# Moving a 64-token sample, and its cached keys and values, from the second super-block of a streaming encoder step to the first

## The chip, the cores and the metric

The kernel runs on one core of one Trainium2 chip. Its time is the device time in microseconds of one execution. The kernel before was run three times: 1246.68, 1248.00 and 1247.45 us, so its median is 1247.45 us.

## What is computed

The reference is one inference step of an encoder layer with two groups of heads that share one input projection. It is applied to 2048 new frames of one stream (the prompt) and, separately, to the next 64 frames of a running stream (the sample), which brings 512 cached rows of keys and values and a recurrent state:

```python
def mixer_layer(x, ln_g, w_in, lb, norm_g, w_out, attn_fn, s0):
    aq, ak, av, ag, hq, hf, hi, hg = jnp.split(rms_norm(x, ln_g) @ w_in, SPLITS, axis=-1)
    o_a = attn_fn(heads(aq), k, v).reshape(B, T, W_A) * jax.nn.silu(ag)
    o_b, S = hgrn2_branch(hq, hf, hi, hg, lb, norm_g, s0)
    y = x + jnp.concatenate([o_a, o_b], axis=-1) @ w_out
```

Group A is attention with 8 heads of 64: each chunk of 64 frames sees its own chunk and the 8 chunks ahead of it, so a prompt frame needs up to 512 earlier frames' keys and values, and the first 512 frames of the prompt have none before frame 0. The sample's 64 frames see the 512 cached rows and themselves. Group B is a gated linear recurrence with 4 heads of 128, whose gate is `f = lb + (1 - lb) * sigmoid(hf)`. `w_in` has 1024 x 4096 elements and `w_out` 1024 x 1024; everything is float32.

## The kernel before, in words

**Super-blocks and jobs.** The 2048 prompt tokens go through in four super-blocks of 512 (table SUPER, L37). The 64 sample tokens ride with one of them, as columns 512 to 575 of its tokens; before, that is the second. For each super-block the normalised tokens lie transposed in SBUF as a high part xh and a low part xl (the float32 value is split in two, so that three passes of matmuls in the faster float32r form give the product). The 32 jobs of a super-block (JOBS, L46; `project`) are the 32 column tiles of w_in: each runs 24 matmuls (8 contraction tiles, times high by high, low by high, high by low) into one of two PSUM accumulators called acc. A super-block of 512 tokens is one block of 512 columns for most jobs; the first two jobs and the last run in two halves of 256. With 576 tokens every job runs as a block of 256 and one of 320, because 512 columns is the most that one accumulator holds.

**Weights.** In the first super-block each tile of w_in is loaded raw (512 KB, two staging buffers wraw), cast to its high part by VectorE, subtracted to its low part by GpSimd in four pieces of 256 columns (`w_split`), and written to DRAM as 1 MB (wd) for the three super-blocks after it, which only load it (four buffers w). The first four raw tiles are loaded at once at the start: two in the wraw buffers, two in the rooms kd and v, which are not in use yet.

**Start.** `program` loads the gain row, the first four token tiles (three in the xn buffers, the fourth in the room kd), the first weights, and issues short matmuls on constants ("breath", "ident") till the first tokens are there. `x_tile` then does, for a tile of 128 tokens: a sum of squares on ScalarE, two small ScalarE instructions for the reciprocal root, two multiplications on VectorE, eight transposes on TensorE in two groups of four, and, in `x_split`, for each group a cast to xh on ScalarE and a subtraction to xl on VectorE. The first two jobs (hq and hf of head 0) are run by halves: half 0 of both, then half 1 of both. Half 1 needs all tiles of tokens from 256 on. `forget_bounds` computes lb and 1 - lb from lb_gamma in a handful of small instructions; the evacuation of hf (`ev_f`) uses them.

**Attention of a pair of heads** (`pair_jobs`, `attention`): kd holds 512 carried key columns and then the block's own, v four carried tiles of values and then the block's own. From the second super-block on, the carried part is loaded from DRAM (`carry`), where the super-block before had stored it. kd and v have one buffer each; the token `kv` passes them from pair to pair. In the first super-block their carried part is not used. For the sample, `sample_cache` loads the pair's cached keys and values (two transfers of 256 KB), transposes the keys on TensorE and splits both; before, it puts them in the two wraw buffers, which are free from the second super-block on. `sample_a` then attends with the sample's rows, after the pair's own blocks.

**Order.** All engines are scheduled by hand: generators (threads) yield a condition or a time, and the class Plan keeps a clock of its own with costs per instruction, resumes whichever thread is ready by that clock, and so writes out the order in which each engine's queue is filled. When the program runs, each engine works through its queue in that order, with semaphores where operands demand it. SyncE's queue holds nearly all DMA issues, in the same manner.

**The end.** The output projection (w_out in seven products per pair of 256-token blocks) fills the last part; the sample's rows are read back from DRAM (mixd) and projected there (`sample_load`, `out_sample`).

## Time and profile before

| What | Value |
|---|---|
| median of three runs | 1247.45 us (1246.68 to 1248.00) |
| span of the profiled execution, first to last instruction | 1244.9 us |
| TensorE: matmul busy, share of span | 1230.1 us, 99% |
| VectorE | 889.3 us, 71% |
| ScalarE | 701.5 us, 56% |
| GpSimd | 372.8 us, 30% |
| DMA | 273.29 MB, mean 220 GB/s |

The profiled execution is shown by its span; around it lies what the timed figure holds besides, 2.55 us if the profiled execution was like the median run. PE is TensorE's matmul queue, PEld its weight loads, DVE VectorE, ACT ScalarE, POOL GpSimd, SP SyncE (SPq its queue of DMA issues). A row of a group reads: engine, operation, output <- inputs by the program's names, shapes, count | busy us, mean ns of one | idle time of the engine just before them and what ended it. A row of the timeline reads: start, duration of the run of instructions, engine, operation, count, and in brackets the idle time before it with its releaser. A matmul's duration holds its way through the array; matmuls follow one another in less than that, so a pace is read from the starts of runs. All instructions of a queue have line L266, the helper that records them, so groups go by the names of tiles.

By the matmuls' names and starts, the first super-block's jobs run from 10 to 239 us, the second's to 546, the third's to 806 and the last one's to 1056.

### The profile page before, as it was taken

How to read it: one execution, taken by the hardware profiler on the slowest of the kernel's cores; microseconds unless marked ns; L12 is line 12 of the kernel's file. 1: busy time of each engine (PE TensorE's matmuls, PEld its weight loads, DVE VectorE, ACT ScalarE, POOL GpSimd, SP SyncE). 2: the span in 40 equal slices, each digit the busy share in tenths (PEclk: the TensorE clock that was granted, in tenths of full speed). 3: DMA queues.
4: the chain of work that ended last, by engine and by line, in shares of the span. 5: the costliest groups of instructions: out<-in, count | busy, mean ns of one | idle time of the engine just before them, and what ended most of it. 6: DMA issues, size and time to landing. Idle time of an engine off the chain costs nothing.

```text
span 1244.9 us, 22078 instructions
## 1 busy us (share of the span) xinstructions
PE 1230.1 (99%) x8068; PEld 1078.4 (87%) x8068; DVE 889.3 (71%) x1863; ACT 701.5 (56%) x1535; POOL 372.8 (30%) x699
## 2 busy tenths in 40 slices
PE   9999999999999999999999999999999999999997
PEld 8788888999999999998888888998888888888786
DVE  7678769776857578586584748683848574787886
ACT  6353556665655557575565657763636455644443
POOL 7757565111120210202543535100101204441110
PEclk9999999999999999999999999999999999999999
DMA  7788698645353553636859595846463656896431
GB/s 295 257 299 298 228 334 330 223 153 183 142 194 137 203 186 145 215 127 239 277 209 333 211 365 213 290 155 213 137 225 116 227 197 269 310 316 201 128 135 68
DMA packets 95406, 273.29 MB, mean 220 GB/s; under 512 B 10369, under 2 KB 43137, under 8 KB 77634
## 3 DMA queue, kind: packets, MB, share of 16 engines
q1 hardware_dynamic: 95154, 271.62, 62.0%
q8 instruction: 64, 1.05, 0.3%
q14 instruction: 44, 0.36, 0.1%
q10 hardware_dynamic: 144, 0.26, 0.1%
HBM read 188.23 MB, written 85.19 MB: 220 GB/s over the span
## 4 chain that ended last, share of the span: by engine, by line
PE 76%; DVE 5%; issue 2%; DMA 2%; ACT 2%; POOL 1%; SPq 0%; DVEq 0%; ACTq 0%; POOLq 0%
PE acc L266 55%; PE g L266 6%; PE tr L266 5%; PE pv L266 5%; PE s L266 5%; DMA wraw<-in_w_in_dram 1%; DVE xn L266 1%; DVE pr L266 1%; POOL w L266 1%; DMA xn<-in_x_prompt_dram 1%; ACT ck L266 0%; DVE q L266 0%; DMA So<-in_state_hgrn_dram 0%; DVE k L266 0%; ACT sig L266 0%
## 5 line engine op out<-in xcount | busy, mean ns | idle before, releaser
L266 PE MATMUL acc<-xh,w 128*128 128x512 f32 (+2 forms) x2688 | 567.2, 349 | 1.5 <-ACT sig L266 0.8
L266 PEld LDWEIGHTS acc<-xh,w 128*128 128x128 f32 x2688 | 434.4, 189 | 52.5 <-DVE gq L266 1.1
L266 PE MATMUL acc<-xl,w 128*128 128x512 f32 (+2 forms) x1344 | 296.2, 350 | 0.0
L266 PEld LDWEIGHTS acc<-xl,w 128*128 128x128 f32 x1344 | 217.2, 189 | 24.8
L266 DVE CUSTOM_DVE_ANT_0 pr<-s,bias 128x640 f32<-128x640 f32 (+5 forms) x144 | 100.8, 704 | 34.1 <-PE s L266 33.6
L266 ACT ACTIVATE pr<-pr,nm 128x640 f32<-128x640 f32 (+4 forms) x132 | 100.6, 763 | 40.6 <-DVE nm L266 39.6
L266 ACT CAST ph<-tr 128x512 fp32r<-128x512 f32 (+3 forms) x176 | 88.2, 507 | 62.4 <-PE tr L266 33.7
L266 POOL TENSOR_TENSOR w<-wraw,w 128x256 fp32r<-128x256 f32 x120 | 105.2, 906 | 54.4 <-issue 22.4
L266 POOL TENSOR_TENSOR mixa<-mixa,sga 128x256 f32<-128x256 f32 (+1 forms) x36 | 28.1, 783 | 308.5 <-DVE mixa L266 267.0
L266 DVE TENSOR_TENSOR ph<-tr,ph 128x512 fp32r<-128x512 f32 (+3 forms) x176 | 100.6, 590 | 8.6 <-ACT ph L266 7.4
L266 PE MATMUL pv<-ph,v 128*128 128x256 f32 (+2 forms) x344 | 95.7, 370 | 0.5 <-DVE ph L266 0.5
L266 PE MATMUL tr<-ident,pr 128*128 128x128 f32 x580 | 90.6, 273 | 0.4 <-DVE sig L266 0.2
L266 PEld LDWEIGHTS tr<-ident,pr 128*128 128x128 f32 x580 | 70.9, 140 | 13.7 <-issue 2.2
L266 ACT ACTIVATE sig<-acc 128x256 f32<-128x256 f32 (+2 forms) x86 | 42.7, 497 | 61.7 <-PE acc L266 61.5
L266 DVE TENSOR_SCALAR pr<-pr,sm 128x640 f32<-128x640 f32 (+4 forms) x132 | 72.9, 552 | 4.7
L266 ACT COPY vT<-acc 128x512 f32<-128x512 f32 (+2 forms) x62 | 31.0, 500 | 75.8 <-PE acc L266 75.7
L266 DVE TENSOR_TENSOR mixa<-mixa,pv 64x256 f32<-64x256 f32 (+1 forms) x144 | 56.9, 395 | 20.6 <-ACT mixa L266 16.4
L266 PEld LDWEIGHTS pv<-ph,v 128*128 128x128 f32 x344 | 58.2, 189 | 7.2 <-DVE ph L266 0.9
L266 ACT ACTIVATE sig<-sig 128x512 f32<-128x512 f32 (+2 forms) x109 | 57.4, 528 | 9.9 <-DVE gk L266 7.1
L266 POOL TENSOR_TENSOR xn<-wraw,xn 128x256 fp32r<-128x256 f32 x48 | 37.1, 792 | 69.5 <-ACT xn L266 69.5
L266 PE MATMUL s<-kd,q 128*128 128x320 f32 (+3 forms) x232 | 56.8, 315 | 0.4
L266 PE MATMUL s<-kd,ql 128*128 128x320 f32 (+3 forms) x232 | 55.5, 309 | 0.0
(314 smaller groups left out, 2041.8 us busy)
## 6 DMA issues: line engine op xcount, KB each, us to landing
w<-wd SPq DMA_DIRECT2D x96, 1024.0 KB, 5.0
wd<-w SPq DMA_DIRECT2D x32, 1024.0 KB, 7.7
wraw<-in_w_in_dram SPq DMA_DIRECT2D x30, 512.0 KB, 5.7
wod<-xn SPq DMA_DIRECT2D x28, 512.0 KB, 5.5
xn<-in_x_prompt_dram SPq DMA_DIRECT2D x23, 512.0 KB, 5.8
bias<-biasd SPq DMA_DIRECT2D x12, 640.0 KB, 7.0
carry<-kd SPq DMA_DIRECT2D x12, 512.0 KB, 6.2
carry<-v SPq DMA_DIRECT2D x12, 512.0 KB, 6.5
```

Source lines behind the costliest of these rows:

```text
L266: r = f(*args, **kw)
```

## The change

SUPER gives the first super-block 576 tokens and the second 512. What belongs to the sample follows: its tokens are a fifth tile of 64 rows at the start, loaded into a part of the room v; its cached keys and values go into the carried parts of kd and v (columns 0 to 511 and tiles 0 to 3) in place of the two wraw buffers; the output stage reads them from mixd[0]. `ev_f` waits, in the plan, till lb and 1 - lb have been issued ("forget") where it waited for an earlier step of theirs ("bounds"). The gain of a tile with 64 rows is cut to 64 rows.

```diff
 SUPER = [
-    (0, 512, [(0, 512)], [(0, 256), (256, 256)]),
-    (512, 576, [(0, 256), (256, 320)], [(0, 256), (256, 320)]),
+    (0, 576, [(0, 256), (256, 320)], [(0, 256), (256, 320)]),
+    (512, 512, [(0, 512)], [(0, 256), (256, 256)]),
     (1024, 512, [(0, 512)], [(0, 256), (256, 256)]),
     (1536, 512, [(0, 512)], [(0, 256), (256, 256)]),
 ]
...
         dve.tensor_scalar(oml, lb, -1.0, 1.0, ALU.mult, ALU.add)
+        have.add("forget")
         sp.dma_start(g_norm, hg_norm_g)
...
-            g = gain[k0 // 4] if gain else g_in[:rows]
+            g = gain[k0 // 4][:rows] if gain else g_in[:rows]
...
     def sample_cache(d):
         p = d.p
-        yield from tk["raw"].get()
-        yield from tk["raw"].get()
-        kc = T(px, [P, 2, 512], F32R, "wraw", bufs=RAWB)
-        vc = T(px, [P, 4, 4, 64], F32R, "wraw", bufs=RAWB)
...
-        yield from split_k(pt, kc, 0, 512, t)
+        yield from split_k(pt, d.kd, 0, 512, t)
...
-        yield from split_v(cv, vc, 0, 4, P, tv)
+        yield from split_v(cv, d.v, 0, 4, P, tv)
...
-        spans = [(kc, 0, 512), (kd, 512 + c0, DEC)]
+        spans = [(kd, 0, 512), (kd, 512 + c0, DEC)]
...
-        tk["raw"].put(2)
...
-            yield lambda: "bounds" in have and front()
+            yield lambda: "forget" in have and front()
...
-        sp.dma_start(mr, mixd[1][:, :, WIN : WIN + DEC].rearrange("f p t -> p f t"))
+        sp.dma_start(mr, mixd[0][:, :, WIN : WIN + DEC].rearrange("f p t -> p f t"))
...
-        xr0 = [T(px, [P, D], F32, "xn", bufs=XNB) for _ in range(3)] + [kroom[:, :D]]
+        xr0 = [T(px, [P, D], F32, "xn", bufs=XNB) for _ in range(3)] + [kroom[:, :D], vroom[:, D : 2 * D]]
...
-        for what, i in (("g", 0), ("x", 0), ("x", 1), ("w", 0), ("x", 2), ("w", 1), ("x", 3), ("b", 0), ("w", 2),
-                        ("w", 3)):
+        for what, i in (("g", 0), ("x", 0), ("x", 1), ("w", 0), ("x", 2), ("w", 1), ("x", 3), ("x", 4),
+                        ("b", 0), ("w", 2), ("w", 3)):
...
-                sp.dma_start(xr0[i], x_rows(0, i * P, P))
+                rows = min(P, SUPER[0][1] - i * P)
+                sp.dma_start(xr0[i][:rows], x_rows(0, i * P, rows))
...
-            for c in range(4):
-                C.spawn(x_tile(0, c // 2, c * P, (xr0[c], landed["x", c]), gps), 0)
+            for c in range(5):
+                C.spawn(x_tile(0, min(c // 2, 1), c * P, (xr0[c], landed["x", c]), gps), 0)
```

The program counts 7330 TensorE, 1355 ScalarE and 474 SyncE instructions before and after; VectorE has 1866 in place of 1865 and GpSimd 721 in place of 704, the 17 being short memsets of "breath" that the plan strews between its longer ones. What differs is the order.

**VectorE near the start**, before. xl is the low part of the tokens: xl from tr_313 and tr_325 is the third tile, from g_339 and acc_356 the fourth. lb and oml are the gate's bounds, w_387 and w_403 the weights of the third and fourth job, sig_389 the evacuation of hf's first half.

```order
L266 TENSOR_TENSOR xl_157<-g_339,xh_156 128x4x128
L266 TENSOR_TENSOR lmx_271<-le_272 128x4
L266 RECIPROCAL lmx_271<-lmx_271 128x4
L266 TENSOR_TENSOR lb_84<-le_272,lmx_271 128x4
L266 TENSOR_SCALAR oml_85<-lb_84 128x4
L266 TENSOR_TENSOR xl_157<-acc_356,xh_156 128x4x128
L266 CAST w_387<-kd_169 128x1024
L266 CAST w_403<-v_170 128x1024
L266 TENSOR_SCALAR sig_389<-sig_389,oml_85,lb_84 128x256
L266 TENSOR_SCALAR gk_308<-sig_389 128x256
L266 CAST w_435<-wraw_289 128x1024
```

The same place now. g_346 and acc_389 are the fourth tile, acc_399 and tr_404 the fifth; sig_385, gb_310, bm_411 and bl_412 belong to hf and the recurrence of head 0; w_435 is the third job's weight.

```order
L266 TENSOR_SCALAR oml_85<-lb_84 128x4
L266 TENSOR_SCALAR sig_385<-sig_385,oml_85,lb_84 128x256
L266 TENSOR_SCALAR gk_309<-sig_385 128x256
L266 TENSOR_TENSOR xl_157<-acc_389,xh_156 128x4x128
L266 SCALAR_TENSOR_TENSOR gb_310<-reset_80,sig_385 128x256
L266 TENSOR_TENSOR bm_411<-gb_310 128x256
L266 TENSOR_TENSOR xl_157<-acc_399,xh_156 128x4x64
L266 TENSOR_TENSOR bl_412<-gb_310 128x256
L266 TENSOR_TENSOR xl_157<-tr_404,xh_156 128x4x64
L266 CAST w_435<-kd_169 128x1024
L266 TENSOR_TENSOR q_129_418<-q_129_418,gq_308 128x256
L266 CAST w_448<-v_170 128x1024
```

Five instructions of head 0's gate and recurrence moved from behind the token tiles to between and ahead of them, and the casts of the third and fourth job's weights moved behind all of these.

**GpSimd, a little later**, before: the low parts of the third and fourth job's weights (four pieces each; the first piece of each stands just ahead of these rows).

```order
L266 TENSOR_TENSOR w_387<-kd_169,w_387 128x256
L266 MEMSET breath_69 128x128
L266 TENSOR_TENSOR w_403<-v_170,w_403 128x256
L266 TENSOR_TENSOR w_387<-kd_169,w_387 128x256
L266 TENSOR_TENSOR w_403<-v_170,w_403 128x256
L266 MEMSET breath_69 128x128
L266 TENSOR_TENSOR w_387<-kd_169,w_387 128x256
L266 TENSOR_TENSOR w_403<-v_170,w_403 128x256
```

The same two weights now, w_435 and w_448: three pieces of the first and two of the second stand ahead of these rows, then the small factors of head 0's recurrence (pf, sf, fq, fk, et), of which these are the last.

```order
L266 TENSOR_TENSOR pf_487<-pf_487,eb_422 128x2
L266 TENSOR_TENSOR et_489<-pf_487,eb_422 128x2
L266 COPY sf_488<-eb_422 128x2
L266 MEMSET breath_69 128x128
L266 TENSOR_TENSOR sf_488<-sf_488,eb_422 128x2 x2
L266 COPY fq_490<-eb_422 128x2
L266 MEMSET breath_69 128x128
L266 COPY fk_491<-eb_422 128x2
L266 TENSOR_TENSOR w_435<-kd_169,w_435 128x256
L266 TENSOR_TENSOR w_448<-v_170,w_448 128x256
```

The last piece of the third job's weight now stands behind the recurrence's factors, which before came after the weights of six jobs.

9 lines of the change are left out of this document (4 added, 5 removed).

## The prediction

> **What bounds the kernel now.** I read the page's span first, then the busy time by stage, then TensorE's waits of the first two super-blocks, then the timeline of three engines at the start. The stages are those in which the jobs of the super-blocks run: 18 to 239 us the first without its start, 239 to 546 the second, with the sample, 546 to 806 the third.
>
> ```profile
> span 1244.9 us, 22078 instructions
> ```
> ```profile
> core 0: us, PE busy (x) PEld busy (x) DVE busy (x) ACT busy (x) POOL busy (x), PEclk, DMA share, GB/s
> 18.00:239.00 221.00, 217.71 (x1354) 183.16 (x1354) 171.39 (x322) 112.05 (x229) 133.75 (x203) 1.00 0.78 279
> 239.00:546.00 307.00, 305.44 (x2517) 296.75 (x2516) 220.05 (x568) 191.04 (x466) 45.14 (x155) 1.00 0.50 173
> 546.00:806.00 260.00, 259.08 (x1666) 221.70 (x1665) 174.98 (x360) 162.25 (x344) 100.63 (x170) 1.00 0.74 261
> ```
>
> TensorE is idle for 221.00 - 217.71 = 3.3 us of the first super-block and 1.6 us of the second; no other engine is near it. The DMA share of 0.78 and GpSimd's 134 us in the first (the weights are split there) look like a second limit, so the question is whether TensorE ever waits for a weight. Its waits say no: the releasers are ScalarE and VectorE alone, 0.8 of the 3.3 us right at the start.
>
> ```profile
> PE acc L266 <- ACT sig L266: 0.8, 1, 0.8
> PE acc L266 <- DVE gq L266: 0.7, 1, 0.7
> PE g L266 <- DVE k L266: 0.6, 2, 0.4
> PE g L266 <- DVE asb L266: 0.6, 1, 0.6
> PE g L266 <- DVE xl L266: 0.5, 2, 0.3
> ```
> ```profile
> PE g L266 <- DVE So L266: 0.4, 1, 0.4
> PE g L266 <- ACT gi L266: 0.3, 1, 0.3
> PE tr L266 <- DVE sig L266: 0.2, 1, 0.2
> ```
>
> The first fence is the first super-block, the second the second. The orders before and after hold the same 7330 TensorE instructions of the same sizes: the block of 256 and 320 that the sample asks for moves from one super-block to the other, and so does the sample's attention. TensorE's work is therefore the same, and the change can only move TensorE's waits. Of those there are 4.9 us to be had in both stages; there is no such limit on what can be added.
>
> **The start (A).** Here the change adds to a chain that TensorE already waits for. The rows are the matmuls' pace and the wait, then ScalarE's and VectorE's part of it.
>
> ```profile
> 1.06 2.93 PE L266 MATMUL g<-breath 128*128 128x128 f32 x12 [1.06 <-POOL breath L451]
> 5.75 1.28 PE L266 MATMUL g<-ident 128*128 128x128 f32 x10
> 18.84 1.22 PE L266 MATMUL acc<-xh,w 128*128 128x256 f32 x8 [0.75 <-ACT sig L266]
> 19.90 1.12 PE L266 MATMUL acc<-xl,w 128*128 128x256 f32 x8
> 274.08 1.34 PE L266 MATMUL acc<-xh,w 128*128 128x320 f32 x8
> 275.25 1.33 PE L266 MATMUL acc<-xl,w 128*128 128x320 f32 x8
> ```
> ```profile
> 12.19 1.04 ACT L266 ACTIVATE ck<-kd 128x1024 bf16<-128x1024 f32 x1
> 13.79 0.37 ACT L266 ACTIVATE sig<-acc 128x256 f32<-128x256 f32 x1
> 16.93 0.59 ACT L266 CAST xh<-acc 128x512 fp32r<-128x512 f32 x1 [0.17 <-PE acc L266]
> 18.37 0.41 ACT L266 ACTIVATE sig<-acc 128x256 f32<-128x256 f32 x1
> 19.36 0.42 ACT L266 ACTIVATE sig<-sig 128x256 f32<-128x256 f32 x1
> 21.60 0.42 ACT L266 ACTIVATE sig<-sig 128x256 f32<-128x256 f32 x1 [1.82 <-DVE gk L266]
> ```
> ```profile
> 18.20 0.68 DVE L266 TENSOR_TENSOR xl<-acc,xh 128x512 fp32r<-128x512 f32 x1
> 20.00 0.83 DVE L266 TENSOR_SCALAR sig<-sig,oml,lb 128x256 f32<-128x256 f32 x1
> 20.86 0.71 DVE L266 TENSOR_SCALAR gk<-sig 128x256 f32<-128x256 f32 x1
> 22.78 1.22 DVE L266 TENSOR_TENSOR_SCAN gb<-reset,sig 128x256 f32<-128x256 f32 x1
> ```
> ```profile
> L266 DVE TENSOR_TENSOR_SCAN gb<-reset,sig 128x256 f32<-128x256 f32 x4 | 2.7, 684 | 0.5 <-ACT sig L266 0.5
> L266 DVE TENSOR_TENSOR bm<-gb 128x256 f32<-128x256 f32 x4 | 1.7, 414 | 0.0
> L266 DVE TENSOR_SCALAR sig<-sig,oml,lb 128x256 f32<-128x256 f32 x4 | 1.6, 409 | 0.9 <-ACT sig L266 0.8
> L266 DVE TENSOR_SCALAR gk<-sig 128x256 f32<-128x256 f32 x4 | 1.2, 294 | 0.1
> L266 DVE TENSOR_TENSOR xl<-g,xh 128x256 fp32r<-128x256 f32 x1 | 0.4, 420 | 0.0
> ```
>
> At 18.84 us half 1 of the first two jobs begins, as soon as ScalarE frees an accumulator. After the change half 1 cannot begin before the fifth tile is cast, nor run its low pass before the fifth tile's xl, and by the order five VectorE instructions of head 0 stand among these. Step by step:
> - ScalarE has one token tile more: 13.79 - 12.19 = 1.60 us (as many columns, so as long, though it has 64 rows).
> - hf's first pass (18.37) then starts at 16.93 + 1.60 = 18.53, since the two copies of the gain between are now behind it; its three passes take 19.36 + 0.42 - 18.37 = 1.41, to 19.9 us.
> - VectorE's sig and gk: 0.41 + 0.29 by the second super-block's rows, or 1.57 by the start's (20.00 to 21.57), where GpSimd was working on weights. To 20.7 or 21.5.
> - ScalarE's fourth pass, 0.42: 21.1 or 21.9. Meanwhile VectorE does the fourth tile's xl, 0.6.
> - The scan, 0.68 or 1.22, then bm, 0.41, or twice that with GpSimd busy; then the fifth tile's first xl, 0.42; bl as bm; its second xl, 0.42. The low pass on the upper four contraction tiles starts at 23.6 or 25.8 us.
>
> Unhindered it starts 12 matmuls into the half, at 275.25 - 274.08 = 1.17 us for 8 of 320 columns, so 1.75 us in. Half 1 therefore runs as if begun at 21.9 or 24.1 us, 3.0 to 5.2 later than 18.84. Of that 0.9 is no loss: the fifth tile's eight transposes stand there (1.28 us for ten, less a 0.3 drain, is 0.11 each), which before came later in the program. A costs 2.1 to 4.3 us; I take 2.5, nearer the quick end, since by the order GpSimd then waits for VectorE's casts and does not disturb it.
>
> **The third job's weight (B).** Its cast comes right behind that last xl, and by the order one of its four low pieces comes behind the recurrence's factors.
>
> ```profile
> 35.02 0.11 POOL L266 MEMSET pf<- 128x16 f32 x1
> 38.50 3.99 POOL L266 TENSOR_TENSOR w<-wraw,w 128x256 fp32r<-128x256 f32 x4
> L266 POOL TENSOR_TENSOR w<-wraw,w 128x256 fp32r<-128x256 f32 x112 | 99.5, 917 | 53.1 <-issue 22.4 <-DVE w L266 16.5 <-PE s L266 9.1
> ```
>
> From the last xl, GpSimd needs a cast (0.7), five pieces (0.75 to 0.92 each), the factors (38.50 - 35.02 = 3.5) and one piece more: 8.7 to 9.7 us. TensorE gets there after 36 matmuls of 0.146 (5.3 us), 16 of 0.12 and 6 more (2.6): 7.9 us. It waits 0.8 to 1.8; the factors are narrower here (two columns, not four), so nothing is possible. I take 1.0, between 0 and 1.8.
>
> **What is late next, and what goes.** The 0.6 us each that TensorE waits for k and asb are waits in a recurrence. Head 0's inputs now precede the token tiles while TensorE comes later; if the waits are head 0's, they go. I take half of it away, -0.6, between -1.2 and 0 (C).
>
> Beyond the start the first super-block gets the sample's VectorE work: 220.05 - 174.98 = 45 us, in about 307 - 260 = 47 us of added time. VectorE goes from 171 in 221 us (78%) to 216 in 268 (81%), before GpSimd's disturbance:
>
> ```profile
> L266 DVE TENSOR_TENSOR bm<-q,pf 128x512 f32<-128x512 f32 x4 | 4.3, 1087 | 0.0
> ```
> ```profile
> L266 DVE TENSOR_TENSOR bm<-q,pf 128x512 f32<-128x512 f32 x4 | 2.7, 679 | 0.0
> ```
>
> The first is the first super-block, the second the last, where GpSimd is mostly idle. One wait like that for gq, which an accumulator released late caused, is 0.7. I add one, +0.7, between 0 and one for each of four heads, 2.8 (D). The second super-block loses the sample and with it part of its 0.9 us of named waits: -0.5, between -0.9 and 0 (E).
>
> What costs nothing: the cached rows' transfers (2 MB in all) and the fifth tile's now stand in SyncE's queue among the first super-block's weights, and the loads behind them come later; two raw buffers and four split ones lie between such a load and TensorE, which waits for no weight now. If that cover were gone, a load's 5.7 us from issue to landing would be seen as waits for w:
>
> ```profile
> wraw<-in_w_in_dram SPq DMA_DIRECT2D x30, 512.0 KB, 5.7
> ```
>
>  The 17 breath memsets are GpSimd's, with 87 us idle there. The new condition of ev_f holds only the plan's thread, behind which nothing is queued but hf itself. At the start, two weight loads stand behind 0.25 MB more. The ends of the program issue the same.
>
> **Sum.** 2.5 + 1.0 - 0.6 + 0.7 - 0.5 = 3.1 us, between 0.0 and 8.9. The profiled span would be 1248.0; with the 2.55 us by which the median of the runs, 1247.45, is above the span, 1250.6 us.
>
> **Rivals.** 0.2%, 2.5 us, is about what a measurement of this kernel can tell from no change.
> - *Given back.* TensorE comes 3 us later to everything behind the start, so C and the later waits for gq and xl (1.2 us) all vanish, and A is at its low end: 2.1 - 1.2 - 1.2 - 0.5 + 1.0 = 0.2, or 1247.7 us. For it: all these waits have inputs that do not depend on TensorE being late. Against: the wait for gq is for an accumulator that VectorE releases late, and a later TensorE makes VectorE's work no shorter. Chance 0.20.
> - *VectorE becomes the bound of the first super-block.* Two-operand work that took 0.68 us takes 1.09 beside GpSimd; if half of the 45 us grows so, VectorE has 230 of 268 us, and every pair and head brings a wait like gq's: 8 x 0.7 = 5.6 for D, 1255.5 us. It decides when a release of acc or s comes later than the job behind it. Chance 0.15.
> - *Faster.* The first super-block's weight work (GpSimd 134 us, DMA 0.78) is spread over 268 us instead of 221, VectorE is less disturbed per job, and the waits of both stages go, -4.1 without the start's, while the planner's order hides the fifth tile: 1243.4 us. Against: no wait of TensorE now is for a weight, and A is in the order. Chance 0.10.
> - *The clock.* While the first breath matmuls run at 0.21 us each (1.06 to 3.79), the ident ones at 0.11 from 5.75: TensorE starts at half pace for some 4.5 us. Should the longer pause at 20 us bring that back for as long, 2.2 us are added: 1252.8. Nothing in this trace pauses that long once it runs. Chance 0.05.
>
> [...]
>
> **How the numbers follow.** The forecast has 0.50, two thirds of it above 1249.95 us. Slower by over 0.2%: 0.33 + 0.15 + 0.05, rounded to 0.55; within: 0.17 + 0.20 less rounding, 0.34; faster 0.11. The range of 1246.0 to 1256.5 us holds the forecast with its bounds, the first rival and the clock, and most of the second; what it leaves out is the faster rival and the rest, under 2 in 10. The forecast's own range is 1247.5 to 1256.
>
> **What would show it.** Right: in the new profile half 1's first matmuls (320 columns) begin near 22 us with waits for xl or xh of 2 to 4 us in sum; the third job's last low piece is waited for by about 1 us; the waits of the rest sum to the same few tenths per super-block. Wrong: half 1 begins before 20.5 us; a wait for w or DMA in the first super-block; a first super-block whose idle time, outside the first 35 us, is over 6 us; or an end later or earlier by more than the first 40 us account for.

## The result and the profile after

The changed kernel takes 1266.28 us, median of 4 runs (1261.78 to 1266.95), the kernel before beside it 1247.72 (1246.68 to 1249.13). The ratio is 1.0143, with a 95% interval of 1.0124 to 1.0161. A second set of four runs (a_again, below) has a median of 1262.29 and a ratio of 1.0119 (1.0099 to 1.0139). The eight executions lie between 1261.18 and 1267.34, median 1264.2: about 16.5 us more than before. They fall into two groups of four, 1261.2 to 1262.4 and 1266.1 to 1267.3, so a median that differs from 1264.2 by 2 or 3 us says little by itself. The prediction was 1250.6, at most 1256.5.

The profiled execution of the changed kernel took 1261.78 us, the shortest of its four. Its page opens with the span, 15.0 us longer than before:

```profile
span 1259.9 us, 22109 instructions
```

Busy time by stage, in the columns that the prediction shows of before (stretch, its length, PE, PEld, DVE, ACT, POOL, granted clock, DMA share, GB/s). The stages end a little later now:

```profile
18.00:303.00 285.00, 275.21 (x2266) 266.08 (x2265) 230.43 (x562) 162.41 (x412) 145.69 (x305) 0.99 0.68 233
303.00:559.00 256.00, 255.65 (x1645) 219.24 (x1644) 162.40 (x348) 142.62 (x286) 30.70 (x76) 1.00 0.56 192
559.00:822.00 263.00, 261.01 (x1665) 222.13 (x1664) 178.51 (x350) 162.41 (x345) 100.92 (x168) 1.00 0.75 258
```

TensorE was idle for 3.3 us in the first super-block; now it is for 9.8. The second falls from 1.6 to 0.4. The third, in which nothing is moved, goes from 0.9 to 2.0. The granted clock of the first is 0.99, so the idle time is not all that was lost there. TensorE's longest waits have new releasers, a transfer among them:

```profile
PE tr L266 <- DMA ck<-in_cache_attn_k_dram: 3.0, 3, 1.2
PE acc L266 <- DVE w L266: 2.3, 1, 2.3
PE g L266 <- DVE So L266: 2.0, 3, 0.8
PE tr L266 <- DVE ph L266: 1.8, 3, 0.8
PE acc L266 <- ACT xh L266: 1.8, 1, 1.8
```

**The start.** TensorE's timeline: the second job's first matmul waits 2.34 us for its weight, half 1 begins at 24.88 and not near 22, and some groups take twice their pace (8 matmuls of 320 columns took 1.33 us in the rows of before; here 2.36):

```profile
15.93 1.42 PE L266 MATMUL acc<-xh,w 128*128 128x256 f32 x6 [2.34 <-DVE w L266]
24.88 1.44 PE L266 MATMUL acc<-xh,w 128*128 128x320 f32 x8 [1.77 <-ACT xh L266]
26.21 2.36 PE L266 MATMUL acc<-xl,w 128*128 128x320 f32 x8
28.36 1.85 PE L266 MATMUL acc<-xh,w 128*128 128x320 f32 x7
```

VectorE shows why the weight is late: it stands for 3.00 us at its first operation on lbg (the forget gate's bounds, 4 KB), and the weight's cast is the next but one in its queue.

```profile
10.46 1.28 DVE L266 TENSOR_TENSOR xl<-tr,xh 128x512 fp32r<-128x512 f32 x2
14.74 0.16 DVE L266 TENSOR_TENSOR lmx<-lbg 128x4 f32<-128x4 f32 x1 [3.00 <-DMA lbg<-in_lb_gamma_dram]
15.09 0.69 DVE L266 CAST w<-wraw 128x1024 fp32r<-128x1024 f32 x1
```

In the kernel before the same operation ran without a wait, at the moment the load landed:

```profile
11.70 0.16 DVE L266 TENSOR_TENSOR lmx<-lbg 128x4 f32<-128x4 f32 x1
```

SyncE's timeline of the changed kernel shows lbg behind the fifth tile (v<-in_x_sample) and taking twice as long to issue (1.01 us, where before it took 0.46); VectorE's wait for it ends 10 us after the issue:

```profile
4.10 0.57 SPq L266 DMA_DIRECT2D v<-in_x_sample_dram  x1
4.72 1.01 SPq L266 DMA_DIRECT2D lbg<-in_lb_gamma_dram  x1
```

And the granted clock (before the last two columns), in two windows of 4 us:

```profile
14.00:18.00 4.00, 2.08 (x11) 2.11 (x12) 3.22 (x8) 3.71 (x11) 2.14 (x4) 0.77 1.01 405
26.00:30.00 4.00, 4.00 (x18) 3.85 (x17) 4.00 (x8) 2.16 (x6) 2.50 (x3) 0.57 0.01 2
```

The trace's clock events are two stretches at half speed, 16.16 to 19.58 and 26.40 to 29.82 us, 3.41 us each. Work that runs through such a stretch ends 1.7 us later, half of 3.41, by estimate. The trace of before has none between its first 4.3 us and its last 1.6. (Every profile of this case ends with one, over its last 1 to 5 us; these are left out from here on.)

**A measure for the rest.** Waits as listed miss small stalls and the clock. So I summed, over TensorE's 8068 records (as many before as after), the time from each start to the next, less the median for its shape in the kernel before. The shapes sum to 1201.7 us in both kernels (the work is the same, as the prediction says), so the remainder is TensorE's whole loss: 35.4 us before, 50.5 after. Super-blocks are counted from 0 here and in the expectations. By place, in us (added filling matmuls are counted as loss, "rest" is super-blocks 0 and 1 after the first 31 us, the last column super-block 3 and the end; times are medians of the runs):

| kernel | first 31 us | rest of 0 and 1 | super-block 2 | 3 and end | time |
|---|---|---|---|---|---|
| before | 4.7 | 17.3 | 6.5 | 6.9 | 1247.7 |
| after | 11.7 | 22.7 | 9.2 | 7.0 | 1264.2 |
| a_again (its profile) | 11.0 | 22.4 | 9.6 | 6.9 | 1262.3 |
| a_bounds_early | 9.2 | 23.4 | 11.0 | 10.1 | 1263.5 |
| a_fill2 | 9.1 | 23.7 | 10.9 | 7.2 | 1263.1 |
| a_rows_ahead | 11.9 | 25.7 | 9.7 | 7.0 | 1266.5 |
| a_all | 8.2 | 24.2 | 10.5 | 8.6 | 1264.0 |
| a_no_load_wait | 12.0 | 20.9 | 9.9 | 8.3 | 1262.5 |
| a_none_late | 8.2 | 20.7 | 8.4 | 7.2 | 1261.0 |
| a_short_ops | 10.1 | 22.0 | 13.3 | 7.0 | 1257.0 |
| a_stores_free | 10.9 | 21.7 | 6.6 | 6.9 | 1258.7 |
| a_plan_1900 | 11.2 | 30.6 | 6.7 | 7.5 | 1267.1 |
| a_plan_2100 | 10.5 | 24.3 | 7.4 | 7.8 | 1261.5 |
| b_bounds_late | 6.3 | 21.4 | 6.4 | 7.1 | 1253.4 |
| b_plan_1900 | 5.2 | 21.5 | 6.3 | 7.6 | 1251.0 |
| b_plan_2100 | 5.1 | 22.9 | 6.5 | 8.1 | 1252.4 |

So the profiled loss of 15.1 us is 7.0 at the start, 5.4 in the rest of the two super-blocks that the change touches, 2.7 in super-block 2, which it does not touch. Each row of losses is one profiled execution, and one kernel's executions differ by up to 9 us, so a difference of one column counts only where it is large or comes again.

Split at the border of super-blocks 0 and 1, the rest reads: super-block 0 after the first 31 us loses 7.9 us before and 17.1 after, super-block 1 loses 9.4 before and 5.6 after. So about 4 us of loss left super-block 1 with the sample's work, and about 9 came to super-block 0.

### The profile page after: what moved, and what is told of

Read it like the earlier page. It is cut to its first block, busy times and chain, and to the rows that moved or that the text cites. A ratio compares the mean times of both kernels' runs of the same rounds, so it can differ in the third digit from the quotient of the medians.

```text
span 1259.9 us, 22109 instructions
## 1 busy us (share of the span) xinstructions
PE 1236.6 (98%) x8068; PEld 1081.0 (86%) x8068; DVE 890.0 (71%) x1864; ACT 701.7 (56%) x1535; POOL 368.0 (29%) x716
## 4 chain that ended last, share of the span: by engine, by line
PE 74%; DVE 5%; DMA 3%; ACT 1%; issue 1%; POOL 0%; SPq 0%; DVEq 0%; ACTq 0%; POOLq 0%
PE acc L266 53%; PE g L266 6%; PE tr L266 5%; PE pv L266 5%; PE s L266 5%; DVE xn L266 1%; DMA xn<-in_x_prompt_dram 1%; DVE pr L266 1%; DMA wod<-xn 1%; DMA ck<-in_cache_attn_k_dram 1%; DMA So<-in_state_hgrn_dram 1%; ACT ck L266 0%; SPq L266 0%; DVE ph L266 0%; DVE mixa L266 0%
## 5 line engine op out<-in xcount | busy, mean ns | idle before, releaser
L266 ACT CAST ph<-tr 128x512 fp32r<-128x512 f32 (+2 forms) x176 | 88.7, 507 | 71.2 <-PE tr L266 37.5
L266 ACT ACTIVATE pr<-pr,nm 128x640 f32<-128x640 f32 (+3 forms) x132 | 100.8, 764 | 47.0 <-DVE nm L266 46.1
L266 DVE CUSTOM_DVE_ANT_0 pr<-s,bias 128x640 f32<-128x640 f32 (+4 forms) x144 | 100.8, 704 | 27.7 <-PE s L266 27.2
L266 POOL TENSOR_TENSOR w<-wraw,w 128x256 fp32r<-128x256 f32 x120 | 97.6, 839 | 62.9 <-DVE w L266 42.6
L266 DVE TENSOR_TENSOR ph<-tr,ph 128x512 fp32r<-128x512 f32 (+2 forms) x176 | 101.6, 590 | 7.9 <-ACT ph L266 7.1
L266 PE MATMUL pv<-ph,v 128*128 128x512 f32 (+1 forms) x376 | 98.5, 360 | 0.8 <-DVE ph L266 0.5
L266 DVE TENSOR_SCALAR pr<-pr,sm 128x640 f32<-128x640 f32 (+3 forms) x132 | 74.3, 563 | 4.7
L266 PE MATMUL s<-kd,q 128*128 128x320 f32 (+3 forms) x240 | 61.1, 325 | 0.3 <-DVE nm L266 0.2
L266 DVE TENSOR_TENSOR ql<-vT,q 64x512 fp32r<-64x512 f32 (+2 forms) x40 | 28.8, 720 | 41.3 <-ACT q L266 40.6
```

The source lines that it names most:

```text
L266: r = f(*args, **kw)
```

## The experiments

The labels beginning with a are made from the changed kernel, those with b from the kernel before.

### The start: the bounds, the pauses and the clock

**a_again**: no edit.

> The changed kernel itself once more, for a second profile of it. Its first profile is of an execution of 1261.8 us, where the other three took 1266.1 to 1267.0. The theory of the clock (the waits of TensorE in the first 30 us bring stretches of half clock, and their number varies from execution to execution) expects the same waits at the start and in super-block 0, and in a longer execution more stretches of half clock than the two of 3.41 us that the first profile has: 4.7 us more would be two to three more. The rival (the same clock, but longer waits for transfers) expects two stretches and waits for DMA that are some 4 us longer in all.

It took 1262.29 us (1261.18 to 1267.34). The profile has the same waits (2.4 for w, 2.6 for xh, 3.0 for ck, 2.0 for So) and one stretch at half clock, at 25.59 us; the pause of 2.44 us before 15.97 has none behind it, where that of 2.34 us before 15.93 in the first profile has one. Which pause brings a stretch varies from execution to execution. None of the longer executions was profiled, but the mean granted clock of each is on record, and one stretch takes about 0.0014 off it (half of 3.41 us in 1260). Of the first four, 1261.78 and 1266.95 us both have 0.997; of the second four, 1262.40 and 1267.34 both have 0.996. By the rounding, at most 1.3 of these differences of 5 us can be the clock's: the theory does not explain these pairs, and what does is not shown. (The other two long executions have 0.995, which is one or two stretches more.)

**a_bounds_early**:

```
-("x", 3), ("x", 4), ("b", 0), ("w", 2)
+("x", 3), ("b", 0), ("x", 4), ("w", 2)
```

> The changed kernel with the load of the forget gate's bounds (lbg) issued ahead of the fifth tile's, where the kernel before has it. Theory one (the late bounds): in the first profile VectorE waits 3.00 us for lbg, the cast of the second job's weight stands behind that, and TensorE waits 2.34 us for it, after which the clock is at half for 3.41 us. So VectorE no longer waits for lbg (its first operation on it at 11.7 us, not 14.7), TensorE's wait of 2.34 us goes, and so does at least the first stretch at half clock, worth 1.7 us: about 4 us less, 1262; if the second stretch goes too, 1260. Theory two (super-block 0 is crowded, and the start is only its first place): half 1 then simply waits longer for the fifth tile, and the time stays within 1 us of 1266.

1263.52 us (1260.04 to 1265.81), no more than about 1 us less. In the profiled execution VectorE still waits 1.47 us for lbg (13.15 us instead of 14.74), TensorE 0.76 for w instead of 2.34. Half 1 begins at 22.55, as predicted for the fifth tile alone, after a pause of 2.25 us, with half clock at 22.95. Two more stretches stand at 57 and 1105 us, behind pauses of 2.17 (cached keys) and 2.05. Theory one was half right on the waits, which shrink but do not go, and wrong on the yield: the start loses 2.5 us less than in the first profile, and other places lose more.

**b_bounds_late**:

```
-("b", 0), ("w", 2), ("w", 3)
+("w", 2), ("b", 0), ("w", 3)
```

> The kernel before, with the load of lbg issued one place later, behind the third weight of 0.5 MB. In its profile lbg landed 7.6 us after its issue at 4.09 us, and VectorE's first operation on it ran at 11.70 without a wait. Theory one: it lands 1 to 3 us later, VectorE waits for it, TensorE waits for the second job's weight, and the clock may fall to half for 3.41 us after it: slower than before by 1 to 5 us, 1249 to 1252.5. The rival: the load of 4 KB is small, it finds room beside the big ones, and the time stays within 0.5 us of 1247.5.

1253.41 us (1250.47 to 1254.40) against 1248.09, ratio 1.0037 (1.0023 to 1.0051): 5.3 us for one place in SyncE's queue, a little above theory one's range. The start accounts for 1.6 of it (TensorE waits 1.36 for w); 4.1 is in the rest. The edit also made the plan place hundreds of lines of TensorE's order anew, so this is no clean price of lbg. It was the first sign that the order itself has a price.

**a_fill**, then **a_fill2** (the bank that the job itself overwrites, for the first pause):

```
+if n == 0:
+    for _ in range({(1, 0): 9, (0, 256): 7}.get((j, off), 0)):
+        nc.tensor.matmul(spare[0] if off else acc[:, :P], ident, ident, start=True, stop=True)
 mm(acc[:, :bn], w[:, wi, kt, :], ...
```

> The changed kernel with 10 and 8 matmuls of 128 columns on the identity, into a bank that nobody reads, ahead of the two groups before which TensorE waited 2.34 and 1.77 us; the order of all else is the same. They run in the wait and keep TensorE busy. The theory of the clock: the stretches of half clock after 16 us are gone, and the time falls by 3.4 us (two stretches of 3.41 us at half pace) or more, to 1263 or less, though the waits for the data stay. The rival (the clock falls for another reason, or the half-clock stretches lie where TensorE waits anyway): stretches as before, and a time within 1 us of 1266, or later by what the added matmuls take beyond the waits (under 0.5 us).

> The changed kernel with 9 and 7 matmuls of 128 columns on the identity ahead of the second job's first matmul and of half 1's first; the first nine now write the bank that the job itself is about to overwrite, because the bank of the earlier try (a_fill) was still read by VectorE and they waited as well. The order of all else is the same. The theory of the clock: TensorE is busy through both waits, so no stretch at half clock lies between 13 and 32 us, while the waits for the data stay; the profiles of the changed kernel have one or two such stretches of 3.41 us there, so 1.7 to 3.4 us less than the changed kernel's runs (1261 to 1267, median about 1264): 1260 to 1262. The rival (the pauses don't set the clock): stretches as before, no less time.

a_fill is no test of the theory: its first ten matmuls write a bank that VectorE was still reading, waited 2.16 us for that and ran after the pause instead of in it (1266.90 us, 1262.92 to 1269.89). In a_fill2 they run where they should. TensorE's timeline: the fillers run through both waits, the matmuls behind them start without one, and the pace never halves.

```profile
13.40 2.17 PE L753 MATMUL acc<-ident 128*128 128x128 f32 x18
15.32 0.96 PE L266 MATMUL acc<-xh,w 128*128 128x256 f32 x6
20.86 1.83 PE L753 MATMUL s<-ident 128*128 128x128 f32 x14
22.70 1.43 PE L266 MATMUL acc<-xh,w 128*128 128x320 f32 x8
```
```profile
14.00:18.00 4.00, 4.00 (x38) 4.00 (x37) 4.00 (x8) 3.75 (x9) 3.72 (x6) 1.00 1.03 418
26.00:30.00 4.00, 4.00 (x29) 3.98 (x28) 4.00 (x5) 1.47 (x3) 4.00 (x6) 1.00 0.00 0
```

The clock is 1.00 where it was 0.77 and 0.57, and the whole profile has no stretch at half speed until its last 3 us. So in this execution filling the pauses took the half clock away; a_all and a_none_late, below, have none either. The pauses do bring it. Yet the time is 1263.05 us (1262.11 to 1268.56), not 1260 to 1262: TensorE is ahead at 31 us, and gives it back. One place shows how. In the changed kernel's super-block 2, ScalarE waits in its queue for a store of the split output weights, with a softmax behind that:

```profile
689.20 0.41 ACT L266 CAST xn<-wraw 128x256 fp32r<-128x256 f32 x1 [1.44 <-DMA wod<-xn]
689.51 0.83 ACT L266 ACTIVATE pr<-pr,nm 128x640 f32<-128x640 f32 x1
```

In a_fill2 everything comes there 1.5 us earlier, ScalarE's cast still starts at 689.29, and TensorE waits for the softmax:

```profile
689.29 0.40 ACT L266 CAST xn<-wraw 128x256 fp32r<-128x256 f32 x1 [3.01 <-DMA wod<-xn]
```
```profile
691.36 0.55 PE L266 MATMUL tr<-ident,pr 128*128 128x128 f32 x3 [1.82 <-DVE pr L266]
```

**b_stops**, for pauses and the clock by themselves:

```
+stop_at = {97: 1, 100: 2, 103: 3, 106: 4, 109: 5, 112: 6, 115: 7}
+if n == 0 and j in stop_at and off == 0:
+    nc.tensor.matmul(acc[:, :P], ident, ident, start=True, stop=True)
+    nc.scalar.copy(scr[:, :1], acc[:, :1])
+    for _ in range(stop_at[j]):
+        nc.gpsimd.tensor_copy(scr, scr)
+    nc.tensor.matmul(acc[:, :P], ident, scr, start=True, stop=True)
```

> The kernel before, with seven made pauses of TensorE in super-block 3, each ahead of a projection: a matmul waits for a copy of a 128 by 128 tile that GpSimd repeats 1 to 7 times, which gives pauses of some 1 to 4 us. Read are the lengths of the pauses and the stretches at half clock behind them. The theory of the clock: pauses of 1.8 us and more bring a stretch of 3.41 us (8 of the 9 pauses of 1.8 to 2.7 us in the first five profiles stand ahead of one, and none of those up to 1.4 us), so about five stretches, which cost 1.7 us each beside the pauses. The rival (the clock falls only behind a pause as long as the stretch itself): stretches only behind pauses over 3.4 us, one at most.

1269.29 us (1268.80 to 1271.53). Four of the seven pauses, from TensorE's timeline:

```profile
899.04 0.49 PE L757 MATMUL acc<-scr,ident 128*128 128x128 f32 x2 [1.82 <-POOL scr L756]
927.95 0.49 PE L757 MATMUL acc<-scr,ident 128*128 128x128 f32 x2 [2.66 <-POOL scr L756]
949.28 0.49 PE L757 MATMUL acc<-scr,ident 128*128 128x128 f32 x2 [2.58 <-POOL scr L756]
983.72 0.49 PE L757 MATMUL acc<-scr,ident 128*128 128x128 f32 x2 [3.54 <-POOL pf L266]
```

Stretches at half clock follow at 950.34 and 984.47 us, behind 2.58 and 3.54. None follows 0.60, 1.01, 1.37, 1.82, nor 2.66. So neither theory holds: there are two stretches, not five and not one, and a pause of 2.58 has one where one of 2.66 has none. Over all 20 profiles of this case (the two pauses of 13.6 us of a_landing and b_landing, below, left out), pauses of 1.2 to 1.75 us stand ahead of a half-clock stretch 3 times in 22, those of 1.75 to 2.1 us 7 times in 15, those of 2.1 to 3.7 us 19 times in 22.

### The cached rows and the sample's state

**a_rows_ahead** (the added lines stand at the start of the recurrence's block, and the load leaves its old place):

```
-        t = C.dma(300)
+        t = C.dma(300) + 3000.0
-        tv = C.dma(300)
+        tv = C.dma(300) + 3000.0
...
+        if bn % P:
+            old = T(pg, [P, P], F32, "So", bufs=2)
+            sp.dma_start(old, state_in[h])
+            held = old, C.dma(64)
```

> The changed kernel with the sample's recurrence state loaded when its block of the recurrence starts, and with the transposes of the cached keys and the split of the cached values planned 3 us later behind their loads. The theory of the cached rows: in the changed kernel's profile TensorE waits 3.0 us in three places for cached keys to land and 2.0 us in three places for the sample's state, all in super-block 0; both go, and the time falls by 3 to 5 us, to 1259 to 1261. The rival (the engines' queues are late there anyway): other waits of the same size take their place, and the time stays within 1 us of the changed kernel's median of about 1264.

1266.46 us (1264.78 to 1267.95). TensorE no longer waits for ck, and for So 0.9 us instead of 2.0, but the rest of super-blocks 0 and 1 loses 25.7 instead of 22.7: waits for gq (2.3), k (1.7) and asb (1.4) stand in their place. Hundreds of lines of TensorE's order differ, so the run can't say whether these waits were there all along or are the new order's.

**a_all**: a_bounds_early and a_rows_ahead together, and 8 fillers ahead of half 1.

> The changed kernel with the bounds' load ahead of the fifth tile's, the sample's state and the cached rows as in a_rows_ahead, and 8 filling matmuls ahead of half 1. If the three theories hold and their costs add (about 2 for the bounds' wait, 3 to 5 for the cached rows and the state, 1.7 to 3.4 for the clock): 1264 less 7 to 10, 1254 to 1257, with at most one stretch at half clock. If the costs are one and the same wait that only moves: 1260 or more.

1264.02 us (1262.96 to 1265.44): the costs don't add. Its start is nevertheless the cleanest measure of the fifth tile: no wait for lbg (11.92 us), no half clock, half 1 at 21.68, and a loss of 8.2 us against 4.7 before. The fifth tile by itself costs 3.5 us.

**a_no_load_wait** keeps each instruction in its place and takes the data away instead:

```
-transpose(pt[...], ck[:, j, :], ident)
+transpose(pt[...], ident, ident)
-dve.scalar_tensor_tensor(new, old, et[...], kv[...], ...)
+dve.scalar_tensor_tensor(new, ident, et[...], kv[...], ...)
-mm(og[...], old, qh[...], ...)
+mm(og[...], ident, qh[...], ...)
```

> The changed kernel with every instruction in the same place, but the identity in place of the cached keys (in the 16 transposes) and in place of the sample's old state (in four VectorE instructions and eight matmuls); both are still loaded. It leaves the cached keys and the old state out of the computation. TensorE and VectorE then have nothing to wait for there. The theory of the cached rows: the waits of 3.0 and 2.0 us in super-block 0 (6.0 us by the matmuls' pace: ck 3.5, asb 2.5) go and nothing takes their place: TensorE's loss in super-block 0 after the first 31 us falls from 17.1 to some 11 us, and the time by 5 to 6 us, from a median of about 1264 to 1258.5. The rival (the engines' queues are late there anyway, as in a_rows_ahead): other waits of the same size come up, in super-block 0 or in super-block 2, and the time falls by less than 2 us.

1262.53 us (1258.97 to 1263.38). The rest of 0 and 1 loses 20.9 us instead of 22.7: 1.8, not 6. The keys' 3.5 us went; the wait named So stayed, though its instruction no longer reads a load:

```profile
PE acc L268 <- DVE w L268: 2.9, 1, 2.9
PE g L268 <- DVE So L268: 2.4, 2, 1.5
```

VectorE's timeline ahead of that wait: a cast waits 1.18 us for its raw weight, and from there VectorE works without a gap through 8 us of query and key splits until So, for which TensorE stands 1.53 us, to 74.67:

```profile
65.97 0.69 DVE L268 CAST w<-wraw 128x1024 fp32r<-128x1024 f32 x1 [1.18 <-DMA wraw<-in_w_in_dram]
67.89 0.93 DVE L268 TENSOR_TENSOR ql<-vT,q 64x320 fp32r<-64x320 f32 x1
71.70 0.87 DVE L268 TENSOR_TENSOR kd<-vT,kd 64x256 fp32r<-64x256 f32 x2
73.55 0.69 DVE L268 TENSOR_TENSOR kd<-tr,kd 64x512 fp32r<-64x512 f32 x1
74.27 0.35 DVE L268 SCALAR_TENSOR_TENSOR So<-ident,et,g 128x128 f32<-128x128 f32 x1
```
```profile
74.67 0.49 PE L268 MATMUL g<-asb,gi 128*128 128x128 f32 x2 [1.53 <-DVE So L268]
```

**a_none_late**: the same, a constant for lbg, and 8 fillers ahead of half 1.

> As a_no_load_wait, and a constant in place of lbg in the forget gate's bounds, and 8 filling matmuls ahead of half 1; the order of all else is the changed kernel's. It leaves the cached keys, the old state and the bounds' values out. If the losses are the three loads' waits and the clock, and add: of the 16 us that the changed kernel lost, 2.3 (the wait behind the bounds), 2 to 3.5 (the clock) and 6 go, and 3 to 5 stay (term A and super-block 2): 1251 to 1253. If earlier work only waits later: 1257 or more, with super-block 2 longer than the 263.3 us of the changed kernel.

1260.95 us (1255.70 to 1263.49): of 11 to 13 us that were to go, about 3 went in the median. The profiled execution is the fastest, 1255.70 us, with no half clock and 44.5 us of loss, 6.0 less than the changed kernel. The start has its 3.5 us and no more; the rest of 0 and 1 still loses 3.4 more than before, super-block 2 1.9 more.

### The order itself

**a_landing** and **b_landing**; then **b_plan_1900**, **b_plan_2100**, **a_plan_1900**, **a_plan_2100**, with 1900.0 and 2100.0 in the same place:

```
-self.landed = end = self.links + 2000.0
+self.landed = end = self.links + 4000.0
```

> The changed kernel with one number of the plan changed: a transfer is planned to land 4.0 us after its bytes are through, not 2.0, so that whatever reads it is placed later in its engine's queue. The measured times from issue to landing are 4.3 to 8 us. The theory that the order is what costs (operations stand in their engine's queue ahead of where their data comes): the waits of TensorE for cached keys, of VectorE for lbg and of ScalarE for the stores of the output weights become fewer, and the time falls by 3 us or more, to 1261 or less. The rival (every new order of this plan brings other waits of its own): 1263 to 1270.

> The same number changed in the kernel before, as the control: 1291 lines of TensorE's order differ, and no work does. If a new order by itself brings new waits, it is slower than before by some us, 1250 to 1258, though no row or load has moved to another super-block. If the order has slack, 1246.5 to 1249.

1290.61 us (1288.82 to 1292.04) and 1281.64 (1281.46 to 1282.07). Both expectations missed by far: a later planned landing, meant to be nearer to the measured ones, gives far worse orders. (By the profile of before, the median time from issue to landing lies between 1.4 and 11.8 us, depending on the transfer, so no single number fits.) In both, one pause of 13.6 us dominates. In a_landing it is at the start of super-block 2, whose later token tiles stand behind the output weights' split in ScalarE's queue:

```profile
602.53 1.12 PE L266 MATMUL g<-ident,xn 128*128 128x128 f32 x4 [13.60 <-DVE xn L266]
```

That says how much hangs on the order, and that the theory behind a_landing (operations placed too early are what costs) is no guide to a better one.

> The kernel before, planned with 1.9 us instead of 2.0 for a transfer's landing. Nothing else differs, but 546 lines of TensorE's order do. The theory of the fitted order (the kernel before stands at a good point of its plan, and any new order costs some us): slower than before by 3 us or more, 1250.5 to 1256. The theory of the moved rows (the loss is the sample's work in super-block 0): within 2 us of before, 1246 to 1249.5.

> The same with 2.1 us: 1082 lines of TensorE's order differ. The theory of the fitted order: 1250.5 to 1258. The theory of the moved rows: 1246 to 1249.5.

> The changed kernel, planned with 1.9 us: 907 lines of TensorE's order differ. The theory of the fitted order: the changed kernel has no good point to lose; it scatters around its 1264, 1258 to 1270. The theory of the moved rows: within 2 us of 1264.

> The changed kernel, planned with 2.1 us: 759 lines of TensorE's order differ. The theory of the fitted order: 1258 to 1270, another time than with 1.9. The theory of the moved rows: within 2 us of 1264.

The kernel before took 1251.04 us (1250.48 to 1251.92; ratio 1.0022, 1.0013 to 1.0031) and 1252.38 (1250.80 to 1255.83; 1.0036, 1.0023 to 1.0050): 0.1 us in one number of the plan costs it 3.1 and 4.5 us, with all rows and loads where they were. The changed kernel took 1267.11 (1264.60 to 1267.86) and 1261.50 (1258.18 to 1263.45); it scatters around its time. In the table, both b runs lose 4.2 to 5.6 us more in the rest of super-blocks 0 and 1 than the kernel before, at most 0.5 at the start and nothing in super-block 2. In b_plan_2100 the largest part is one pause of 3.55 us at 243 us, where super-block 1 begins, with a half-clock stretch behind it. The a runs lose 6.7 and 7.4 in super-block 2 where the changed kernel loses 9.2 and the kernel before 6.5. And every order of the changed kernel whose start was left as it is loses 10.1 us or more there, and the two new ones wait for cached keys as well (5.6 and 2.8 us). In super-block 0 after the first 31 us, the four orders made from the kernel before (itself, b_bounds_late, b_plan_1900 and b_plan_2100) lose 8 to 12 us, with a pause at its end counted in, and every one of the changed kernel 15 or more. Both theories hold a part: the b runs speak for the fitted order, the start, the keys and super-block 0 for the moved rows.

### What is left

**a_short_ops**: a_no_load_wait with 58 of VectorE's operations narrowed in super-block 0.

```
-dve.tensor_scalar(s[:, :nk], s[:, :nk], sm, None, ALU.mult)
+dve.tensor_scalar(s[:, :16], s[:, :16], sm, None, ALU.mult)
-dve.tensor_mul(q0[:, :bn], q0[:, :bn], qs[:, c])        (and k0, k1)
+dve.tensor_mul(q0[:, :16], q0[:, :16], qs[:, c][:, :16])
```

> a_no_load_wait with 58 of VectorE's in-place operations in super-block 0 (the softmax's scaling and three products of the recurrence) done on 16 columns only; no instruction is moved or left out. Beside what a_no_load_wait leaves out, it leaves out most of these products. The operations take 30.8 us in a_no_load_wait, and would take some 10. The theory of the crowded VectorE (it comes late to what TensorE waits for): TensorE's loss in super-block 0 after the first 31 us falls from 15.2 us towards the 8 to 11 that the kernel before has in its super-block 0, and the time by 4 to 6 us from that kernel's median of 1262.5, to 1257 to 1258.5. The rival (the waits come from the order of the queues, whatever the operations take): the loss stays at 14 to 15 us and the time within 1.5 us.

1257.01 us (1254.48 to 1263.64), 5.5 less than a_no_load_wait: that is what the crowded VectorE was to give. Five of the six executions lie below every one of a_no_load_wait's. Their granted clocks, 0.997 and 0.998 where those have 0.995 to 0.997, make about 2 us of it, by an estimate from the means. But the profiled execution is the sixth and slowest, and it does not show the loss going: 22.0 us in the rest of 0 and 1 (1.7 of it a half-clock stretch at 74.8 us), against 20.9. VectorE's busy time fell by 12.8 us there, from 230.65 to 217.89:

```profile
18.00:301.00 283.00, 274.46 (x2263) 266.17 (x2261) 217.89 (x562) 161.96 (x413) 142.10 (x305) 0.99 0.68 233
```

The times speak for the crowded VectorE and the one trace does not, so whether VectorE's load sets super-block 0's loss is left open.

**a_stores_free**:

```
-sp.dma_start(wod[i][:, :, a], st.rearrange("p (h c) -> p h c", h=2))
+sp.dma_start(wod[i][:, :, a], g_in.rearrange("p (h c) -> p h c", h=2))
```

> The changed kernel in its own order, with the stores of the split output weights taking a constant tile, so that no split waits for an earlier store to have left its stage tile. It leaves the output weights' values out. In the changed kernel's super-block 2 ScalarE waits 8.4 us in 4 places for these stores, with the softmax's operations queued behind it. The theory (these waits are what makes super-block 2 longer): its length falls from 263.3 to about 261, TensorE's loss there from 9.2 to about 6.5 us, and the time by 2 to 3 us from about 1264, to 1261 to 1262. The rival (they are hidden, as most of ScalarE's waits are): 263 us and 1264, as before.

1258.68 us (1257.41 to 1259.56), every execution below all eight of the changed kernel. Super-block 2's loss is 6.6 us, as before the change (6.5), and its length 260.7 us:

```profile
559.00:820.00 261.00, 260.03 (x1669) 222.96 (x1668) 179.31 (x351) 163.10 (x346) 102.08 (x168) 1.00 0.76 260
```

So the 2.7 us of super-block 2 are ScalarE standing at the output weights' stores, with the softmax behind it. That wait exists in both kernels (7.3 us of ScalarE's time before, 8.4 after); of these two orders only the changed one lets TensorE run out of work meanwhile, and a_plan_1900 and a_plan_2100 lose little there (6.7 and 7.4). The rest of the 5.5 us gained on the median of 1264.2 is 1.8 us in the first 31 us and the rest of 0 and 1, and what the executions differ by.

## Why the prediction was wrong

The direction was right, the reason for most of the loss was not named. In the prediction's terms, with what the profiles showed (15.1 us in all):

| term | forecast | measured |
|---|---|---|
| the start: A | 2.5 | 3.5 |
| the start: the third load behind the fifth tile, and the clock | 0 | 3.5 |
| the cached rows and the state | 0 | 1.8 |
| the rest of super-blocks 0 and 1: B, C, D and E | 0.6 | 3.6 |
| super-block 2 | 0 | 2.7 |

So 8 of the 12 us that the forecast lacks stand in terms that it put at nothing.

- **The start (A)**: right, within its bounds. The prediction says "I take 2.5", between 2.1 and 4.3; the fifth tile by itself costs 3.5 (a_all, a_none_late). Half 1 was to begin near 22 us: 21.68 in a_all, 22.55 in a_bounds_early, 24.88 in the changed kernel, where the late bounds come first.
- **"At the start, two weight loads stand behind 0.25 MB more"**: this step failed. Behind the fifth tile stands a third load, lbg, which had no slack: in the kernel before it landed just as VectorE came for it. These 4 KB, 3.00 us late, held VectorE's queue, the second job's weight and TensorE (2.34). With the clock below, it makes 3.5 of the start's 7.0 us (11.7 less 8.2).
- **The clock** (rival, 0.05): it happened, in every profile of the changed kernel and its variants but the three whose fillers ran in the pauses. "Nothing in this trace pauses that long once it runs" is true of the trace before, whose longest pause there is 0.75 us, but the change itself makes the pauses: 1.8 to 2.6 us were enough, which is A's own size, so the price belonged into A. The price, 2.2 us, is about right for one stretch (1.7); the changed kernel has one or two at the start, and others have more at later pauses.
- **B**: it did not come. No wait for the third job's weight shows in the changed kernel, in which TensorE comes to it later.
- **C**: its condition held. The waits of 0.43 us for k and 0.57 for asb, at 39.66 and 43.73 us of the kernel before, have no counterpart in either profile of the changed kernel, in which TensorE's next wait behind half 1 is the one for cached keys at 57 us.
- **"What costs nothing: the cached rows' transfers"**: wrong by 3.0 us of waits. "Two raw buffers and four split ones lie between such a load and TensorE" is true of weights. Cached keys have one buffer and go from it straight to TensorE. SyncE's timeline has their load behind a weight's store and the bias's rows, and taking 1.47 us to issue; TensorE takes what has landed at once:

```profile
44.63 1.91 SPq L266 DMA_DIRECT2D wd<-w  x1
47.96 1.47 SPq L266 DMA_DIRECT2D ck<-in_cache_attn_k_dram  x1
```
```profile
57.26 0.66 PE L266 MATMUL tr<-ident,ck 128*128 128x128 f32 x4 [1.00 <-DMA ck<-in_cache_attn_k_dram]
```

  Taken away with the order kept, keys and state give 1.8 us net.
- **D and E** (+0.7 and -0.5): with the loads' waits gone, the rest of super-blocks 0 and 1 still loses 3.6 us more than before (20.9 against 17.3). E had the right sign and was too small: the second super-block alone loses 9.4 before and 5.6 after, with the sample's work gone, where E's bound was -0.9. D, with a bound of 2.8, was mis-sized by more: super-block 0 loses 7.9 before and 15.2 with the loads' waits gone, which is 7.3 more. How much of this is VectorE's load is open; its backlog is seen ahead of So, but a_short_ops settles it neither way.
- **The unspoken step: an order is as good as another where no term stands.** "The change can only move TensorE's waits" is true and bounds nothing. The kernel before stands at a good point of its plan: new orders without any change cost 3.1 and 4.5 us. The net 3.6 us above are of that size, and super-block 2's 2.7 go with the order, by the a_plan runs and a_stores_free. Super-block 0's 7.3 are more than the new orders without a change cost there (about 4 at most), which speaks for the moved work; no run isolates it.
- **Given back**: the prediction's first rival has a mechanism that works on the other side. The loss is not absorbed later, but what a repair gains is, in good part (a_fill2, a_all, a_none_late).

The prediction's own test had said it: "a wait for w or DMA in the first super-block" and idle time over 6 us outside the first 35 would be wrong, and both are there. Open are the scatter of the changed kernel's executions (1261 to 1267, where before has 1246 to 1251; by the granted clocks, half-clock stretches explain only a part), the rest of super-block 0, and a better order: no version here comes near the kernel before.

## What to carry to other kernels

Before calling a moved load free, list all that is queued behind it down to the smallest, and ask of each how long its reader's queue could still wait: a load that just makes it has no slack, and one small operand stops an engine's queue with all that stands behind it (here 4 KB cost VectorE 3.00 us and TensorE 2.34). A TensorE pause of 2 us in a kernel that is otherwise dense must be priced with the half-clock stretch that may follow (here 3.41 us long, 1.7 us lost). Where a planner orders the queues and its numbers were fitted to one arrangement, measure what a new order costs by itself (a small change of one plan number, in the old arrangement) and put that into the range.

## What the runs showed of the hardware

- In the 20 profiles, the two pauses of 13.6 us left out, a stretch at half clock stood behind 19 of 22 pauses of TensorE between 2.1 and 3.7 us, 7 of 15 between 1.75 and 2.1, and 3 of 22 between 1.2 and 1.75. The length alone did not settle it: in b_stops a pause of 2.58 us had one behind it and one of 2.66 had none. The two stretches in the changed kernel's profile lasted 3.41 us each and began 10.24 us apart (16.16 and 26.40), the two of b_stops 34.13 us apart (950.34 and 984.47). Why a stretch begins where it does is not shown.
- A load of 4 KB among the first loads took 7.6 us from issue to landing in the kernel before (up to 8.2 in its variants that keep the place), and 10 us one place further back in the changed kernel (8.4 to 10.6 in its variants, by the end of VectorE's wait). The place is not all: back in its old place with the fifth tile's load behind it, it took 7.8 us in a_all and 9.0 in a_bounds_early.
- Keeping TensorE busy with matmuls that nobody reads kept the clock at 1.00 through waits of 2.3 and 1.8 us in the profiled execution of a_fill2. They must write a bank that is free by then: a_fill's first ones waited 2.16 us themselves, for VectorE.
